# Loading the output weights earlier, and the norm weights and two rows of x later, at the end of attention

## The chip, the cores and the metric

The kernel runs on one core of one Trainium2 chip. The metric is the time of one execution on the device in microseconds (us). TensorE multiplies, VectorE, ScalarE and GpSimd (POOL) work on vectors, and SyncE's queue (SP) issues nearly all transfers between the chip's memory and the core's on-chip memory.

## The reference

One layer of a decoder on 2048 tokens of width 1024, in float32. Cut to what matters here:

```python
nx = rmsnorm(h, attn_norm_g[l])
proj = jnp.einsum('bsd,dp->bsp', nx, w_in[l])
...
o_a = gla_mixer(...)                       # gated linear attention, 4 heads
o_a = o_a * lax.rsqrt(...) * gla_norm_g * jax.nn.silu(gr)
o_b = dilated_mixer(dq, dk_, dv_, rel_bias)  # 8 heads, three branches each, combined
mixed = jnp.concatenate([o_a, o_b], axis=-1)
h = h + jnp.einsum('bsm,md->bsd', mixed, w_out[l])

nm = rmsnorm(h, mlp_norm_g[l])
a = jnp.square(jax.nn.relu(jnp.einsum('bsd,df->bsf', nm, w_ff1[l])))
h = h + jnp.einsum('bsf,fd->bsd', a, w_ff2[l])
return rmsnorm(h, final_norm_g)
```

## The kernel before

Five stages follow one another: the input projection, attention, the output product (from 897 us), the first MLP product and the second MLP product. The big products are done in float32 through three products of split operands: a value is rounded to a high part by ScalarE (`A.activation(..., AF.Copy)`), VectorE subtracts it from the value to get the low part, and TensorE multiplies high by high, low by high and high by low (`mm3`, lines 65 to 68). Whatever enters such a product as a weight needs a load, a ScalarE copy and a VectorE subtraction first; for the output weights these are lines 899, 900 and 901 in `load_wo`, once for each of eight blocks of 128 rows.

**Attention** runs over 160 units, made from 4 pairs of heads, 2 heads in each and 3 branches (dilations 16, 4 and 1) of each head. A unit is four blocks of 128 queries in the branch of dilation 16 and two in the others. The loop does one turn for each unit in a pipeline: the scores of the unit three turns ahead (lines 659 and 661, then bias and minimum on VectorE in line 671 and the exponential on ScalarE in line 672), the transposes of the unit of this turn (line 681, copied out by ScalarE in 688 or VectorE in 690), and the product with v of the unit two turns back (line 700, copied out in 703). The gated linear attention (GLA, lines 827 to 889) goes along in small steps. For the branches of dilation 16 and 4, q is packed by POOL first (`pack_q`, line 613). When a pair of heads is done with a branch its result goes to memory (`boD`, line 777); when all three are done, the rows are loaded again (`combine_load`, line 725, tile `cmb`) and combined by weights (`combine`, lines 737 to 760), by POOL for the first three pairs and half by POOL, half by VectorE for the last. Combined rows and GLA's rows go to `mixD`, also through line 777, except those of the last pair for the first eight tiles, which are read from their tile `O`.

Work that belongs to a certain turn is registered with `at_unit` and done ahead of that turn's own work. `load_wo` is registered for the eight turns 132, 135, ..., 153.

**Output product.** `mix_T(t)` loads the mixer rows (line 1073) and the rows of x (line 1074) of a tile of 128 tokens into a tile `mx`, transposes the mixer rows (line 377) and splits them into `mT`. Tiles are taken in the order 0, 4, 1, 5, ... The next tile's `mix_T` stands ahead of this tile's product. The first two tiles are multiplied in two halves, chunks 0 to 3 and then 4 to 7. Line 1184 adds the rows of x to the product, and `norm_to_T` norms the sum with the repeated row `gM`. The other repeated row, `gF`, is used by `output` at the end of the second MLP product (lines 1268 and 1272).

**Who sets the order.** The first part of the kernel has its order written out by hand. From line 536 on the framework's scheduler arranges each engine's instructions when the kernel is compiled, by a model of the time and with the order of the program as the priority; `keep_in_program_order` pins an instruction behind what stands ahead of it on its engine. On the chip each engine's stream is then fixed, and an instruction that has to wait holds up what stands behind it on its engine; SP's queue is such a stream too. All large tiles (`slot`) are of one size and come from one ring of 25 buffers; a new tile takes the place of one that has seen its last use, and waits for that use.

Of the kernel before, what the change touches and what calls it, by code (L numbers as in the profile page):

```python
# [18 lines left out]
D = 1024  # L19
# [11 lines left out]
AHEAD, LAG = 3, 2  # L31
# [9 lines left out]
def emit(tc, a, stop=99):  # L41
    nc = tc.nc
    V, A, G, T, SP = nc.vector, nc.scalar, nc.gpsimd, nc.tensor, nc.sync
# [6 lines left out]
    def ps(tag):  # L50
        return psum.tile([128, 512], F32, name="ps_" + tag, tag=tag, bufs=BANKS[tag])

    def slot(name, dt=F32, n=SLOT):

        return up.tile([128, SLOT], dt, name=name, tag="u", bufs=25)[:, :n]

    def view(t, shape):
        n = int(np.prod(shape))
        names = "abcd"[:len(shape)]
        return t[:, :n].rearrange(f"p ({' '.join(names)}) -> p {' '.join(names)}", **dict(zip(names, shape)))  # L60

    def bcast_row(ap, n):
        return bass.AP(tensor=ap.tensor, offset=ap.offset, ap=[[0, 128], [1, n]])

    def mm3(out, sh, sl, mh, ml, first, last):
        T.matmul(out, sh, mh, start=first, stop=False)  # L66
        T.matmul(out, sl, mh, start=False, stop=False)  # L67
        T.matmul(out, sh, ml, start=False, stop=last)  # L68
# [82 lines left out]
    x2 = a["x"].rearrange("o s d -> (o s) d")  # L151
# [198 lines left out]
    def split(hi, lo, src):  # L350
        A.activation(hi, src, AF.Copy)  # L351
        V.tensor_tensor(lo, src, hi.bitcast(F32), op=OP.subtract)  # L352
# [18 lines left out]
    def transposed(xt, last=None, pin=False, by=ident):  # L371
        out = []
        for q in range(2):
            pv = view(ps("cd"[q]), (4, 128))
            for k in range(4):
                of = xt[:, (4 * q + k) * 128:(4 * q + k + 1) * 128]
                ins = T.transpose(pv[:, k, :], last if last is not None and 4 * q + k == 7 else of, by)
                if pin and q + k == 0:
                    tc.keep_in_program_order(ins)
            out.append(pv)  # L380
        return out
# [78 lines left out]
    def reload(n):  # L460

        j, cs = order[n // 2], slice(1024 * (n % 2), 1024 * (n % 2) + 1024)
        t = (xp, bp)[n // 2 % 2][:, cs]
        SP.dma_start(t, nTD[j - 1].rearrange("p c s -> p (c s)")[:, cs])

        def rest():
            hi, lo = [v[:, cs] for v in TF[j]]
            tc.keep_in_program_order(A.activation(hi, t, AF.Copy))
            V.tensor_tensor(lo, t, hi.bitcast(F32), op=OP.subtract)
            if n + 4 < 14:  # L470
                back.append(reload(n + 4))

        return rest
# [418 lines left out]
    wo = a["w_out"].rearrange("o (c p) n -> p (o c) n", p=128)  # L892
    WO = []

    def load_wo(n):
        for c in range(len(WO), len(WO) + n):
            raw = slot("woraw")[:, :D]
            w = view(slot("wo", FR), (2, D))
            SP.dma_start(raw, wo[:, c])
            A.activation(w[:, 0], raw, AF.Copy)  # L900
            V.tensor_tensor(w[:, 1], raw, w[:, 0].bitcast(F32), op=OP.subtract)
            WO.append(w)
# [35 lines left out]
    def at_unit(n, *f):  # L938
        plan.setdefault(n, []).append(f)
# [44 lines left out]
            was = b  # L984
    NU = len(units)
    for i in range(8):
        at_unit(NU - 28 + 3 * i + AHEAD, load_wo, 1)
    gla = gla_steps()
    for k in range(-AHEAD, NU + LAG):
# [3 lines left out]
        if 0 <= k - LAG:  # L993
            u = units[k - LAG]
            u.b.v = vs[u.b.h // 2, u.b.br]
            pv = u.values()
        if k + AHEAD < NU:
            u = units[k + AHEAD]
# [9 lines left out]
        if 0 <= k - LAG:  # L1008
            u = units[k - LAG]
# [14 lines left out]

    gs = slot("gs")
    gM, gF = gs[:, :D], gs[:, D:2 * D]
    SP.dma_start(gM, bcast_row(a["mlp_norm_g"], D))
    SP.dma_start(gF, bcast_row(a["final_norm_g"], D))
    bb, tb = slot("bb"), slot("tb")
    rb, TF, TB = [slot("rb")], {}, {}  # L1030

# [37 lines left out]
    def mix_T(t):  # L1069
        u = view(slot("mx"), (2, D))  # L1070
        to = D - 128 if t < 8 else D
        for cs in (slice(0, 512), slice(512, to)) if t in (0, 4) else (slice(0, to),):
            SP.dma_start(u[:, 0, cs], mixD[t * 128:t * 128 + 128, cs])
        SP.dma_start(u[:, 1], x2[t * 128:t * 128 + 128])
        m = view(slot("mT", FR), (2, CH, 128))
        for q, pv in enumerate(transposed(u[:, 0], outs[3, 0][:, t, 1:129] if t < 8 else None)):
            split(*[m[:, i, 4 * q:4 * q + 4] for i in range(2)], pv)
        return u, m
# [38 lines left out]
    def bank():  # L1117
        tags.append(tags.pop(0))
        return ps(tags[-1])

    def product1(at):
        g, j = jobs1[at]
        half, gh = divmod(g, NP)
        if not acc1:
            acc = [slot("acc1") for _ in range(4)]
            acc1.extend(t[:, 512 * q:512 * q + 512] for t in acc for q in range(4))
        X, c11, c12, c21, c22, s2, s4 = acc1[7 * (g % 2):7 * (g % 2) + 7]
        p = bank()
        B, W = TB[j], combs1[at % 4]
        for c in range(4):  # L1130
            mm3(p, W[:, 0, c], W[:, 1, c], B[0][:, c], B[1][:, c], c == 0, c == 3)

        def square(v):
            A.activation(v, v, AF.Relu)  # L1134
            A.activation(v, v, AF.Square)

        def store(q, n, v):
            q.dma_start(actD[n - 1, half, gh], v)

        if j in (1, 5, 4):  # L1140
            A.activation({1: X, 5: c22, 4: c21}[j], p, AF.Copy)
        elif j == 2:
            V.tensor_tensor(c11, p, X, op=OP.add)
            square(c11)
            store(A, 1, c11)
        elif j == 6:
            V.tensor_tensor(X, p, X, op=OP.add)
            V.tensor_tensor(c12, X, c22, op=OP.add)
        elif j == 3:
            V.tensor_tensor(c12, p, c12, op=OP.add)  # L1150
            square(c12)
        else:
            V.tensor_tensor(X, p, X, op=OP.add)
            V.tensor_tensor(c21, c21, X, op=OP.add)  # L1154
            V.tensor_tensor(c22, c22, X, op=OP.add)
            square(c22)
            square(c21)
            store(SP, 4, c22)
            store(SP, 2, c21)
            V.tensor_tensor(X, c12, c22, op=OP.add)  # L1160
            V.tensor_tensor(s2, X, c11, op=OP.subtract)
            V.tensor_tensor(c12, c11, c12, op=OP.subtract)
            V.tensor_tensor(s4, c21, s2, op=OP.subtract)
            for n, v in ((5, X), (6, s2), (7, c12), (3, s4)):
                store(SP, n, v)

    tiles = [8 * half + i + 4 * k for half in range(2) for i in range(4) for k in range(2)]
    nxt = mix_T(tiles[0])
    late = None
    back = []  # L1170
    for at, t in enumerate(tiles):
        u, m = nxt
        if at + 1 < NT:
            nxt = mix_T(tiles[at + 1])
        h = u[:, 1]
        p = [ps("a"), ps("a")]
        parts_ = 2 if at < 2 else 1
        for q in range(parts_):
            for n in range(2):
                cs = slice(n * 512, n * 512 + 512)  # L1180
                for c in range(q * CH // parts_, (q + 1) * CH // parts_):
                    mm3(p[n], m[:, 0, c], m[:, 1, c], WO[c][:, 0, cs], WO[c][:, 1, cs], c == 0, c == CH - 1)
                if q == parts_ - 1:
                    V.tensor_tensor(h[:, cs], p[n], u[:, 1, cs], op=OP.add)
        SP.dma_start(hD[t * 128:t * 128 + 128], h)
        if late is not None:
            norm_to_T(*late)
        if back:
            list(back.pop())
        if at in RELOAD:  # L1190
            back.append(reload(order[at - RELOAD[0]], 0))
        if at == W1AT:
            load_w1(0)
        if at == W1AT + 1:
            prep1(0)
            prep1(1)
        late = (h, u[:, 0], t)
# [144 lines left out]
    for at in range(7, len(jobs1)):  # L1342
        if at == first - 2:
            halves.update({n: reload(order[n], 1) for n in range(2)})
        prep1(at + 2)
        product1(at)
        for n in parts_at.get(at, ()):
            next(halves[n])
            if n in begun and n + 2 < 7:
                halves[n + 2] = reload(order[n + 2], 1)  # L1350
            begun.add(n)
        if at == len(jobs1) - 6:
            for n in range(2):
                load_b(n)
                load_a(n)
        if at in (len(jobs1) - 4, len(jobs1) - 2):
            n = (at + 4 - len(jobs1)) // 2
            prep_b(n)
            prep_a(n)
# [3 lines left out]
    for ph, (j, half) in enumerate(phases):  # L1363
        P = [bank() for _ in range(4)]
        for k in range(8):
            n = 8 * ph + k
            prep_a(n + 2)
            at = k + 8 * (1 - half)
# [72 lines left out]
```

## Time and profile before

| what | value |
|---|---|
| median of 3 runs | 2332.82 us (2329.7 to 2334.34) |
| the profiled execution's own time | 2333.23 us |
| its span, first to last instruction | 2331.4 us |
| instructions | 34990 |
| mean granted TensorE clock | 0.993 |
| transfers | 457.59 MB, 196 GB/s on average |

The profile is one execution. Its page gives the busy time of each engine (PE is TensorE, PEld its weight loads, DVE VectorE, ACT ScalarE, SPq SyncE's queue), and the trace behind it can be asked for stretches of time, for the instructions in order, and for who waited for whom. In a row of the timeline stand the start in us, the duration, the engine, the line of the kernel, the operation with its tiles (out<-in), and in brackets the idle time of the engine just before it and what ended it. In a row of waits stand the waiting engine with its tile and line, the releaser, and the us in total, the number of waits and the longest. In a table of stretches each engine has its busy time and, in brackets, the number of its instructions; the last three columns are the granted TensorE clock (1.00 is full), the busy share of the transfer engines, and GB/s. In a tile's answer a row has the durations in ns (least/median/greatest) and the first and last start.

### The profile page before, as it was taken

The page shows a single profiled execution, that of the slowest core. Times are in us where ns is not written, and L with a number is a line of the kernel's source. Part 1 is how long each engine was busy: PE and PEld are TensorE (multiplying, and loading weights), DVE is VectorE, ACT ScalarE, POOL GpSimd, SP SyncE. Part 2 cuts the span into 40 slices and gives each one's busy share as a digit, 9 for nine tenths or more (in the row PEclk, how much of TensorE's full clock was granted, in tenths as well). Part 3 has the DMA queues.
Part 4 walks back from the last instruction along what each step waited for, and adds up shares of the span by engine and source line. Part 5 has one row for each costly group of instructions (what it writes and reads, how often), then busy time and mean ns, then how long its engine had stood idle before and what let it go on. Part 6 is the DMA issues. An engine that isn't in the chain of part 4 may idle for free.

```text
span 2331.4 us, 34990 instructions
## 1 busy us (share of the span) xinstructions
PE 2289.2 (98%) x12652; PEld 1978.2 (85%) x12652; DVE 1572.1 (67%) x2926; ACT 1146.1 (49%) x2200; POOL 434.2 (19%) x530
## 2 busy tenths in 40 slices
PE   6999999999999999999999999999999999999998
PEld 6977999789999998888888887888888888888886
DVE  7978778776677677445877779777764356446545
ACT  5665446535677673224555566555544223224324
POOL 0133103235377685000000000000000100001002
PEclk9999999999999999999999999999999999999999
DMA  4457754777676855678644447444476487457643
GB/s 152 143 159 239 219 179 127 215 224 237 199 234 210 279 181 187 196 229 277 200 158 155 157 149 269 165 153 156 155 266 230 164 284 251 139 170 261 209 162 108
DMA packets 341804, 457.59 MB, mean 196 GB/s; under 512 B 18117, under 2 KB 214230, under 8 KB 336256
## 3 DMA queue, kind: packets, MB, share of 16 engines
q1 hardware_dynamic: 336878, 446.71, 59.0%
q10 hardware_dynamic: 4754, 8.66, 1.0%
q8 instruction: 99, 1.62, 0.3%
q14 instruction: 73, 0.60, 0.1%
HBM read 292.99 MB, written 167.02 MB: 197 GB/s over the span
## 4 chain that ended last, share of the span: by engine, by line
PE 76%; DVE 2%; DMA 1%; POOL 1%; issue 1%; ACT 1%; SPq 0%; POOLq 0%; DVEq 0%; ACTq 0%
PE ps_a L66 8%; PE ps_a L68 8%; PE ps_a L67 8%; PE ps_c L66 7%; PE ps_c L67 7%; PE ps_c L68 7%; PE ps_d L66 4%; PE ps_d L68 4%; PE ps_d L67 4%; PE ps_a L700 4%; PE ps_o L67 3%; PE ps_o L68 2%; PE ps_o L66 2%; PE ps_d L681 2%; PE ps_c L659 2%; PE ps_c L661 2%
## 5 line engine op out<-in xcount | busy, mean ns | idle before, releaser
L352 DVE TENSOR_TENSOR ca<-ra,ca 128x1024 fp32r<-128x1024 f32 x112 | 137.8, 1231 | 157.5 <-ACT ca L351 157.4
L1268 POOL TENSOR_TENSOR suma<-suma,gs 128x512 f32<-128x512 f32 x16 | 23.3, 1471 | 1144.0 <-ACT scr L1266 1143.9
L351 ACT ACTIVATE ca<-ra 128x1024 fp32r<-128x1024 f32 x112 | 118.0, 1053 | 220.3 <-PE ps_c L68 176.0
L351 ACT ACTIVATE w1comb<-w1raw 128x512 fp32r<-128x512 f32 x224 | 139.7, 627 | 151.8 <-PE ps_c L68 54.6
L352 DVE TENSOR_TENSOR w1comb<-w1raw,w1comb 128x512 fp32r<-128x512 f32 x224 | 154.0, 690 | 49.5 <-ACT w1comb L351 49.2
L672 ACT ACTIVATE pe<-pe,O 128x256 f32<-128x256 f32 (+1 forms) x384 | 156.0, 454 | 61.3 <-DVE O L671 58.1
L700 PE MATMUL ps_a<-v,pt 128*128 128x65 f32 x1200 | 179.7, 253 | 2.4 <-DVE pt L690 2.0
L700 PEld LDWEIGHTS ps_a<-v,pt 128*128 128x128 f32 x1200 | 176.4, 195 | 5.0 <-DVE pt L690 2.6
L681 PE MATMUL ps_d<-ident,pe 128*128 128x128 f32 x600 | 158.5, 279 | 1.1 <-ACT pt L688 1.1
L671 DVE CUSTOM_DVE_ANT_0 pe<-ps_c,nb 128x256 f32<-128x256 f32 (+1 forms) x384 | 126.3, 361 | 37.6 <-PE ps_d L681 15.2
L206 ACT ACTIVATE wcomb<-wraw 128x512 fp32r<-128x512 f32 (+2 forms) x126 | 96.6, 774 | 94.1 <-PE ps_o L67 19.5
L351 ACT ACTIVATE cb<-rb 128x1024 fp32r<-128x1024 f32 x56 | 59.4, 1061 | 163.7 <-PE ps_o L67 105.0
L67 PE MATMUL ps_c<-hb,w1comb 128*128 128x512 f32 x336 | 131.0, 390 | 0.1
L66 PE MATMUL ps_c<-hb,w1comb 128*128 128x512 f32 x336 | 130.8, 389 | 0.0
L68 PE MATMUL ps_c<-hb,w1comb 128*128 128x512 f32 x336 | 130.7, 389 | 0.0
L66 PE MATMUL ps_c<-cb,ca 128*128 128x512 f32 x336 | 130.7, 389 | 0.0
L67 PE MATMUL ps_c<-cb,ca 128*128 128x512 f32 x336 | 130.7, 389 | 0.0
L68 PE MATMUL ps_c<-cb,ca 128*128 128x512 f32 x336 | 130.7, 389 | 0.0
L208 DVE TENSOR_TENSOR wcomb<-wraw,wcomb 128x512 fp32r<-128x512 f32 (+2 forms) x84 | 90.2, 1075 | 31.0 <-ACT wcomb L206 30.8
L681 PEld LDWEIGHTS ps_d<-ident,pe 128*128 128x128 f32 x600 | 108.8, 186 | 1.7 <-ACT pt L688 1.3
L352 DVE TENSOR_TENSOR cb<-rb,cb 128x1024 fp32r<-128x1024 f32 x56 | 68.2, 1222 | 60.6 <-ACT cb L351 60.5
L1134 ACT ACTIVATE acc<-acc 128x512 f32<-128x512 f32 x128 | 79.6, 631 | 52.8 <-DVE acc L1154 34.8
(392 smaller groups left out, 7158.4 us busy)
## 6 DMA issues: line engine op xcount, KB each, us to landing
ra<-actD SPq DMA_DIRECT2D x56, 1024.0 KB, 7.0
actD<-acc SPq DMA_DIRECT2D x192, 256.0 KB, 2.4
rb<-w_ff SPq DMA_DIRECT2D x72, 512.0 KB, 4.5
w1raw<-w_ff SPq DMA_DIRECT2D x32, 1024.0 KB, 5.7
k<-kD SPq DMA_DIRECT2D x16, 1024.0 KB, 8.0
rb<-hTD SPq DMA_DIRECT2D x13, 1024.0 KB, 6.0
wraw<-w_in SPq DMA_DIRECT2D x48, 256.0 KB, 4.1
cmb<-boD SPq DMA_DIRECT2D x16, 528.0 KB, 5.6
```

Of the source, the lines that this page charges most:

```text
L66: T.matmul(out, sh, mh, start=first, stop=False)
L67: T.matmul(out, sl, mh, start=False, stop=False)
L68: T.matmul(out, sh, ml, start=False, stop=last)
L206: A.activation(hi, src, AF.Copy, scale=sc)
L208: V.tensor_tensor(lo, src, hi.bitcast(F32), op=OP.subtract)
L351: A.activation(hi, src, AF.Copy)
L352: V.tensor_tensor(lo, src, hi.bitcast(F32), op=OP.subtract)
L671: V.tensor_tensor_reduce(p, s, bias, scale=1.0, scalar=BIG, op0=OP.add, op1=OP.min, accum_out=nm)
L672: A.activation(p, p, AF.Exp, bias=nm, scale=-1.0)
L681: T.transpose(pb[:, i * 128:i * 128 + 128], src, ident)
L700: T.matmul(self.b.opsum[:, n % 4], self.pt[:, i * 128:i * 128 + 128], self.b.v[:, blk, cols], start=first, stop=last)
L1134: A.activation(v, v, AF.Relu)
```

## The change

The load of each block of output weights is taken out of `load_wo` and registered by itself eight turns earlier, so for turns 124, 127, ..., 145. The repeated row `gM` is loaded behind the first tile's `mix_T`, and `gF` in the first MLP product, behind its product number 14, pinned to that place in SP's queue. For the first two tiles (0 and 4) `mix_T` no longer loads the rows of x; they are loaded in the loop, behind the next tile's `mix_T`.

```diff
+    wo_raw = {}
+
+    def raw_wo(c):
+        wo_raw[c] = slot("woraw")[:, :D]
+        SP.dma_start(wo_raw[c], wo[:, c])
+
     def load_wo(n):
         for c in range(len(WO), len(WO) + n):
-            raw = slot("woraw")[:, :D]
+            raw = wo_raw.pop(c)
             w = view(slot("wo", FR), (2, D))
-            SP.dma_start(raw, wo[:, c])
             A.activation(w[:, 0], raw, AF.Copy)
             V.tensor_tensor(w[:, 1], raw, w[:, 0].bitcast(F32), op=OP.subtract)
             WO.append(w)
...
     for i in range(8):
+        at_unit(NU - 36 + 3 * i + AHEAD, raw_wo, i)
         at_unit(NU - 28 + 3 * i + AHEAD, load_wo, 1)
...
     gM, gF = gs[:, :D], gs[:, D:2 * D]
-    SP.dma_start(gM, bcast_row(a["mlp_norm_g"], D))
-    SP.dma_start(gF, bcast_row(a["final_norm_g"], D))
...
-        SP.dma_start(u[:, 1], x2[t * 128:t * 128 + 128])
+        if t not in (0, 4):
+            SP.dma_start(u[:, 1], x2[t * 128:t * 128 + 128])
...
     nxt = mix_T(tiles[0])
+    SP.dma_start(gM, bcast_row(a["mlp_norm_g"], D))
...
         if at + 1 < NT:
             nxt = mix_T(tiles[at + 1])
+        if at < 2:
+            SP.dma_start(u[:, 1], x2[t * 128:t * 128 + 128])
...
         product1(at)
+        if at == 14:
+            tc.keep_in_program_order(SP.dma_start(gF, bcast_row(a["final_norm_g"], D)))
```

## The prediction

> **What bounds the kernel now.** I read the page first: TensorE is busy over the whole span, so time can only be won where it stands or runs slowly. Then a table of stretches around the end of attention, the only place that the change touches before 900 us.
>
> ```profile
> PE 2289.2 (98%) x12652; PEld 1978.2 (85%) x12652; DVE 1572.1 (67%) x2926; ACT 1146.1 (49%) x2200; POOL 434.2 (19%) x530
> ...
> core 0: us, PE busy (x) PEld busy (x) DVE busy (x) ACT busy (x) POOL busy (x), PEclk, DMA share, GB/s
> 840.00:860.00 20.00, 19.93 (x182) 19.52 (x181) 17.35 (x55) 15.79 (x40) 19.84 (x23) 1.00 0.68 223
> ...
> 860.00:865.00 5.00, 3.57 (x33) 3.13 (x32) 2.52 (x10) 3.55 (x10) 5.00 (x5) 1.00 0.79 260
> 865.00:872.00 7.00, 6.75 (x32) 6.08 (x31) 5.92 (x18) 5.09 (x14) 6.68 (x9) 0.51 0.73 186
> ...
> 884.00:890.00 6.00, 4.94 (x40) 4.37 (x40) 6.00 (x10) 3.95 (x13) 6.00 (x5) 1.00 1.03 393
> 890.00:892.40 2.40, 0.63 (x6) 0.39 (x4) 2.40 (x4) 1.09 (x2) 2.24 (x3) 0.98 0.40 155
> 892.40:895.80 3.40, 3.38 (x17) 3.38 (x18) 3.40 (x8) 0.00 (x0) 3.40 (x3) 0.51 0.00 0
> 895.80:905.00 9.20, 9.20 (x62) 8.36 (x62) 6.36 (x13) 2.59 (x6) 8.57 (x18) 1.00 0.45 138
> ```
>
> The columns after the stretch are its length and each engine's busy time. There are two holes. The first: TensorE is idle 5.00 - 3.57 = 1.43 us in 860 to 865 and 0.25 us up to 872, together 1.68, and then works 7.00 us at a granted clock of 0.51, which costs 7.00 x 0.49 = 3.43. Sum **5.11 us**. The second: idle 6.00 - 4.94 = 1.06, 1.77 and 0.02 us, and 3.40 x 0.49 = 1.67 of half clock, **4.52 us**. From these two at most 9.63 us can come. Before and after them the rows have TensorE full.
>
> What ends the first hole is told by the timeline, the queue of SyncE beside it, and the table of waits (us in total, times, longest).
>
> ```profile
> 855.99 0.37 SPq L777 DMA_DIRECT2D mixD<-O  x1
> 856.41 0.57 SPq L899 DMA_DIRECT2D woraw<-w_out  x1
> 859.13 0.37 SPq L777 DMA_DIRECT2D boD<-O  x1
> 859.59 0.42 SPq L899 DMA_DIRECT2D woraw<-w_out  x1
> ...
> 866.58 6.28 SPq L725 DMA_DIRECT2D cmb<-boD  x4
> ...
> 861.42 1.06 ACT L900 ACTIVATE wo<-woraw 128x1024 fp32r<-128x1024 f32 x1 [1.90 <-DMA woraw<-w_out]
> ...
> 866.46 1.04 ACT L900 ACTIVATE wo<-woraw 128x1024 fp32r<-128x1024 f32 x1
> ...
> 862.51 1.51 DVE L901 TENSOR_TENSOR wo<-woraw,wo 128x1024 fp32r<-128x1024 f32 x1 [2.48 <-ACT wo L900]
> ...
> 863.02 0.44 PE L870 MATMUL ps_o<-ident,gla 128*128 128x128 f32 x2 [1.09 <-ACT gla L862]
> ...
> ACT wo L900 <- DMA woraw<-w_out: 4.9, 4, 1.9
> ...
> SPq L899 <- PE ps_c L661: 8.6, 2, 8.3
> ...
> SPq L725 <- DVE wo L901: 3.9, 1, 3.9
> ```
>
> The fifth weight row was issued at 856.41, straight behind the store of a combined pair, and ScalarE reached its split before it landed: 1.90 us of waiting with everything behind it in line (the GLA copy L862, for which TensorE waits). VectorE waits 2.48 us for ScalarE's half, and so do its bias sums and copies of transposed probabilities. Of four such waits (4.9 us) only this one shows in TensorE's rows.
>
> ```profile
> 883.62 1.26 DVE L901 TENSOR_TENSOR wo<-woraw,wo 128x1024 fp32r<-128x1024 f32 x1
> ...
> 887.69 2.93 DVE L758 TENSOR_TENSOR cmb<-cmb,small 128x512 f32<-128x512 f32 x2
> 890.55 1.21 DVE L901 TENSOR_TENSOR wo<-woraw,wo 128x1024 fp32r<-128x1024 f32 x1
> ...
> 892.42 0.69 PE L700 MATMUL ps_a<-v,pt 128*128 128x65 f32 x2 [1.78 <-DVE pt L690]
> ```
>
> The second hole has no transfer in it. VectorE is busy 6.00 of 6.00 and 2.40 of 2.40 us: two late splits and the combination of the last pair stand before the copy that TensorE needs.
>
> **The change part by part.** No arithmetic is added or removed; all of it is order.
>
> *Weight rows eight turns earlier.*
>
> ```profile
> L899 SPq DMA_DIRECT2D woraw<-w_out x8: 333/382/578, 830.0 to 878.9; - x8
> ...
> DMA to landing us min/median/max: 3.5/5.0/5.3
> ```
>
> Eight loads, three turns apart, take 830.0 to 878.9: 48.9 / 21 = 2.33 us a turn, so eight turns are 18.6 us against a landing of at most 5.3. The wait of L900 for its DMA goes in all four places. In the first hole that takes away the cause: 1.68 us idle, and the half clock that follows, 3.43. I take **-5.11**. Bounds: 0, if another wait holds the same split; -5.11 at the other end, since nothing else stands in the rows there. The eight issues (0.38 us each) only change places in SyncE's queue.
>
> The clock is worth a remark, as two thirds of this term are clock. The row shows half clock right behind an idle time of 1.68 us and again behind 1.77. [...]
>
> *What it costs: slots.* Every large tile comes from one ring of 25 slots, and slots are given in program order: the two rows of norm weights, which wait for no data, go out only behind the last weight row.
>
> ```profile
> 876.47 0.58 SPq L899 DMA_DIRECT2D woraw<-w_out  x1
> ...
> 878.86 0.55 SPq L899 DMA_DIRECT2D woraw<-w_out  x1
> 879.65 0.33 SPq L1027 DMA_DIRECT2D gs<-mlp_norm_g  x1
> 880.03 0.50 SPq L1028 DMA_DIRECT2D gs<-final_norm_g  x1
> 880.63 0.93 SPq L1073 DMA_DIRECT2D mx<-mixD  x2
> ```
>
> The ring is full in this stretch. The first weight row waits 8.3 us for the scores to be done with a packed q (L661), and the combine loads L725 wait 3.9 us for a split (L901), that is for a weight row's slot. I count the tiles alive at 866: 4 of GLA, pe, pt, one bias, one v (8), q and two k of both heads (14), the older pair's result and its combine tile (16), the last pair's result (17), six split weights (23), two combine tiles (25). A raw row now lives about eight turns instead of two or three, so two or three more are held. Early on (800 to 830 us) this pushes the packing of q (L613) towards the scores that need it. VectorE and TensorE have three turns of lead there, 7 us, against casts of four parts that can start once the q of the branch before is free; I take **0** and bound it by +1.7, the idle time of the first hole. Near the end the sixth and seventh row hold the slots of the two combine tiles:
>
> ```profile
> 873.21 2.53 POOL L760 TENSOR_TENSOR O<-O,cmb 128x512 f32<-128x512 f32 x2
> ...
> 875.11 0.65 DVE L737 TENSOR_TENSOR small<-O,cmb 128x8 f32<-128x8 f32 x1
> ...
> 895.36 0.42 PE L377 MATMUL ps_d<-ident,O 128*128 128x128 f32 x1
> ...
> 897.72 0.48 PE L66 MATMUL ps_a<-wo,mT 128*128 128x512 f32 x1
> ```
>
> Then L725 has to wait until POOL lets the older combine tile go, at 873.21 + 2.53 = 875.7: up to 875.7 - 866.6 = 9.1 us later. Combining starts at 875.11 and reaches TensorE at 895.36, 20 us, with VectorE and POOL doing other work in between; some of it can close up, and the first tile's first half product (24 matmuls from 897.72) doesn't need it. Bounds: 0 and +9.1; I take **+1.5**, near the low end, since most of the 20 us is queueing.
>
> *Second hole.* If splits wait for no transfer, the last two can run before VectorE is taken up by combining. The two subtractions are 1.26 + 1.21 = 2.47 us, more than the 1.77 us of idle; gone, with their half clock, this is 1.77 + 1.67 = 3.44. If splits bunch up here instead, nothing is won. Half way: **-1.7**; bounds 0 and -3.44.
>
> *Norm weights and x rows later.* 512 KB each for the two repeated rows and for two rows of x leave the place ahead of, or among, the first tiles' mixer rows.
>
> ```profile
> mx<-x SPq DMA_DIRECT2D x2, 512.0 KB, 8.6
> boD<-O SPq DMA_DIRECT2D x2, 528.0 KB, 4.1
> ...
> L1184 DVE TENSOR_TENSOR mx<-ps_a,mx x32: 679/691/692, 911.5 to 1100.3; 128x512 f32<-128x512 f32 x32
> ...
> L1268 POOL TENSOR_TENSOR suma<-suma,gs x16: 1267/1304/2343, 1843.5 to 2324.6; 128x512 f32<-128x512 f32 x16
> ```
>
> The mixer rows land a few us earlier, but TensorE's first transpose of them stands behind other work, not behind a transfer, so this wins **0** by itself; it is what lets a faster attention run on into the product. The x rows are first read at 911.5; issued some 10 us later, by 899, and landing within 8.6, they are in time. If they were not, TensorE still has the next tile's product before it lacks a PSUM bank. The final norm's row is first read at 1843.5 and is now issued early in the first MLP stage, hundreds of us ahead: 0. Bounds for both: 0 and +1.7, one idle of the first hole's size.
>
> **Sum.** -5.11 + 0 + 1.5 - 1.7 + 0 = -5.3. The profiled execution took 2333.23 us (span 2331.4 and 1.8 around it), 0.4 above the median 2332.82; so 2333.23 - 5.3 = 2327.9 in its terms, and **2327.5** beside the median.
>
> **The rivals.**
>
> *The wait moves.* The load is early but the split's own slot isn't free: with the raw rows holding slots, the fifth split needs the one that the store boD<-O at 859.13 gives back when it has landed (4.1 us in the row above), no sooner than the 861.42 at which it ran before. For it: the waits of L899 and L725 on slots; the same store line in front of both. Against: splits are then placed where their slot is free, and may not block ScalarE at the same spot. Nothing net: 2332.8, and 2330 to 2335 around it. This is also how the change would fail to do what it says.
>
> *Slower: the split waits for POOL.* The sixth split's slot comes free only with POOL's last L760 at 875.7, where before its load went out at 859.59 and its split ran at 866.46. If ScalarE's queue reaches it on time, it stands up to 875.7 - 866.5 = 9.2 us, the exponentials behind it; three turns of lead cover little, as the first hole's 1.90 us wait already made 1.68 us idle. That is some 9 us idle and 3.4 us of half clock, less the 5.11 won and part of the second hole: 12.4 - 5.1 - 1 = +6, 2339. It decides from a wait of about 5 us on. For it: POOL is busy 19.84 of 20.00 and 5.00 of 5.00 us in the rows from 840 to 865. Against: a schedule that counts POOL's time puts the split behind it.
>
> *Clock not tied to the gap.* If the half clock came from something else than this idle time, only the idle would go: -1.68 - 0.9 (half of 1.77) + 1.5 = -1.1, 2331.7 beside the median. The rows speak against it: 0.51 stands behind both gaps and nowhere else here. [...]
>
> *Both holes close* and combining isn't late: -5.11 - 3.44 = -8.6, 2324.2.
>
> **How the numbers follow.** The forecast, with both holes' case as its good end, has 0.42; the moved wait 0.25 and the untied clock 0.05, both within 0.2% (about 4.7 us, what a measurement of this kernel can tell from no change); the slower case 0.28. So faster 0.42, same 0.30, slower 0.28. As cases of both signs matter, the range runs from below the best case to the slower case and a little over: 2321 to 2341. The forecast's own range is 2323 to 2331.
>
> **What would show it.** Right: L900 waits for no DMA; TensorE's row for the fifth split has no idle time and the clock stays 1.00 through 865 to 872; the combine loads still come before 870. Wrong: L900 waiting for a store, for PE or for POOL; L725 near 876 and the transposes of O after 900 with idle TensorE before them; the packing of q ending a wait of the scores.

## The result, and the profile after

The changed kernel takes **2340.51 us** in the median of 5 runs (2336.17 to 2342.72), the kernel before 2332.82 (2329.7 to 2334.41, 5 runs). The ratio is **1.0031, 95% interval 1.002 to 1.0043**: some 7 us slower, where 5 us faster was forecast. One execution of a kernel described further down, h1, took 6030.16 us; its ratio leaves that one out. The profiled execution of the changed kernel took 2342.72 us with a span of 2340.9, against 2331.4 before. In its listing the split is in lines 905 (ScalarE) and 906 (VectorE) instead of 900 and 901, and the addition of x in line 1192 instead of 1184; the load is in line 899 of both.

Not all of the 9.5 us between the two spans belongs to the change. The last store that SyncE issues ahead of the first moved load stands in the timeline of its queue at 805.63 before and at 808.07 after:

```profile
805.63 0.36 SPq L777 DMA_DIRECT2D mixD<-O  x1
```

```profile
808.07 0.36 SPq L777 DMA_DIRECT2D mixD<-O  x1
809.10 5.03 SPq L899 DMA_DIRECT2D woraw<-w_out  x1
...
862.70 0.33 SPq L899 DMA_DIRECT2D woraw<-w_out  x1
...
870.74 0.33 SPq L899 DMA_DIRECT2D woraw<-w_out  x1
...
880.60 4.03 SPq L725 DMA_DIRECT2D cmb<-boD  x4
```

So 2.4 us were there before the change could act: up to that place both traces have the same instructions in the same order on every engine. The additions of x, 911.5 to 1100.3 in the row quoted for the forecast, are now here (line 1192's instructions: durations in ns, first and last start):

```profile
L1192 DVE TENSOR_TENSOR mx<-ps_a,mx x32: 675/691/692, 919.1 to 1107.5; 128x512 f32<-128x512 f32 x32
```

The last one is 7.2 us later, so 7.2 - 2.4 = **4.8 us** arose between 808 and 1107; the other 2.3 came behind 1107, where nothing but the one load of `gF` differs in the order of the instructions. What was bought for the 4.8 is in the answer for the tile of raw weights:

```profile
L899 SPq DMA_DIRECT2D woraw<-w_out x8: 332/333/5026, 809.1 to 870.7; - x8
L905 ACT ACTIVATE wo<-woraw x8: 1042/1058/1059, 847.9 to 880.9; 128x1024 fp32r<-128x1024 f32 x8
L906 DVE TENSOR_TENSOR wo<-woraw,wo x8: 1216/1226/2211, 849.0 to 887.0; 128x1024 fp32r<-128x1024 f32 x8
its engine sat idle before it (us, times) until:
  ACT wo L905: 2.0, 3
  DVE wo L906: 1.3, 1
  POOL O L760: 0.3, 1
```

Before, the same answer had the loads at 830.0 to 878.9 and the eight ScalarE halves at 833.5 to 884.4. The first load is 20.9 us earlier, and no split waits for its load any more; yet the **first split is 14.4 us later** (847.9 against 833.5; 2.4 of it is the shift). In the built program the first split went into the place of an old bias tile before. With raw rows ahead of it in the ring, the last packed q now takes that place, and the first split gets the place of this packed q, which the scores read until 846.9. Four splits bunch up at 848 to 861 us. Two stalls follow. The first is in the timeline of VectorE and TensorE:

```profile
859.40 0.43 DVE L703 COPY O<-ps_a 128x260 f32<-128x260 f32 x1 [2.61 <-PE ps_a L700]
860.57 1.28 DVE L906 TENSOR_TENSOR wo<-woraw,wo 128x1024 fp32r<-128x1024 f32 x1 [0.74 <-ACT wo L905]
861.89 0.29 DVE L671 CUSTOM_DVE_ANT_0 pe<-ps_c,nb 128x128 f32<-128x128 f32 x1
...
862.59 0.39 PE L659 MATMUL ps_c<-k,qs 128*128 128x256 f32 x1 [2.94 <-DVE O L671]
```

The row at 861.89 is the first bias sum of the last pair's plain branch (dilation 1); it stood at 852.32 before. Here it stands straight behind the fourth split, and TensorE, whose next scores wait for that sum, is idle for 2.94 us. In the built program the tile `O0`, into which this sum also writes, takes the place of the **fourth raw row**, whose last use is that split; before, it took the third's, which was free much sooner (its split ends at 851.52). The fourth split in turn is written into the place of an old v, released by the product L700 for which VectorE waits in the first row. So the chain is: L700 (it ends at 859.36), split (ScalarE, from 859.50), split (VectorE), bias sum, scores. ScalarE comes to this split only at that time anyway, behind work that itself waited for TensorE (its L862 at 858.56, 3.30 us).

The second stall is where the combination meets the output product. In a table of stretches (length, each engine's busy time, clock):

```profile
845.00:862.60 17.60, 14.42 (x125) 13.73 (x123) 12.53 (x30) 12.53 (x32) 17.44 (x17) 1.00 0.80 283
862.60:880.00 17.40, 17.05 (x150) 16.55 (x151) 15.89 (x56) 14.72 (x36) 17.01 (x18) 1.00 0.57 170
880.00:884.75 4.75, 2.85 (x29) 2.64 (x27) 0.43 (x2) 3.16 (x7) 1.00 (x3) 1.00 0.82 214
884.75:891.60 6.85, 6.28 (x29) 5.91 (x30) 6.19 (x20) 3.95 (x13) 1.84 (x5) 0.50 1.17 327
891.60:903.60 12.00, 10.31 (x97) 9.97 (x96) 11.47 (x33) 6.71 (x21) 9.04 (x19) 1.00 0.64 241
903.60:920.00 16.40, 13.44 (x66) 10.85 (x67) 14.95 (x28) 1.90 (x4) 14.31 (x19) 1.00 0.07 17
```

TensorE's idle time is 3.18 + 0.35 + 1.90 + 0.57 + 1.69 + 2.96 = 10.65 us, and half clock over 6.85 us costs 3.4: 14.1 us, against 9.63 in the two holes before, 4.4 of the 4.8 us. Who ends the later idle times is in the timeline again:

```profile
884.75 0.17 DVE L737 TENSOR_TENSOR small<-O,cmb 128x8 f32<-128x8 f32 x1 [3.84 <-DMA cmb<-boD]
885.32 0.58 PE L659 MATMUL ps_c<-k,qs 128*128 128x256 f32 x1 [2.47 <-DVE O L671]
...
903.54 0.50 PE L66 MATMUL ps_a<-wo,mT 128*128 128x512 f32 x1 [1.69 <-DVE O L703]
...
914.21 3.24 DVE L758 TENSOR_TENSOR cmb<-cmb,gla 128x512 f32<-128x512 f32 x2
917.97 1.16 DVE L760 TENSOR_TENSOR O<-O,cmb 128x512 f32<-128x512 f32 x1
919.06 0.68 DVE L1192 TENSOR_TENSOR mx<-ps_a,mx 128x512 f32<-128x512 f32 x1
...
919.79 0.50 PE L66 MATMUL ps_a<-wo,mT 128*128 128x512 f32 x1 [2.35 <-DVE mx L1192]
```

The combine loads, at 866.58 before, are issued at 880.60, behind the eighth raw row at 870.74. In the built program one of the two combine tiles takes the place of the older pair's result, which its last store has to let go, and the other that of the sixth raw row. In the waits of SyncE's queue this is

```profile
SPq L777 <- POOL O L760: 9.9, 3, 4.3
...
SPq L725 <- DMA mixD<-O: 2.1, 1, 2.1
```

so POOL's combining of the older pair holds up the stores, and the stores hold up the loads. VectorE stands 3.84 us for the loads and holds up the scores at 885.32; then its half of the combination runs at 914 to 919, ahead of the first addition of x, and TensorE waits 2.35 us for that addition, which reads a finished product out of the memory that TensorE writes (PSUM).

### The profile page after: what moved, and what is told of

Its sections match the earlier page's. It is cut to its first block, busy times and chain, and to the rows that moved or that the text cites. A ratio compares the mean times of both kernels' runs of the same rounds, so it can differ in the third digit from the quotient of the medians.

```text
span 2340.9 us, 34995 instructions
## 1 busy us (share of the span) xinstructions
PE 2290.9 (98%) x12652; PEld 1978.5 (85%) x12652; DVE 1570.6 (67%) x2926; ACT 1145.7 (49%) x2200; POOL 432.0 (18%) x530
## 4 chain that ended last, share of the span: by engine, by line
PE 48%; DVE 1%; DMA 1%; ACT 1%; issue 0%; POOL 0%; POOLq 0%; SPq 0%; DVEq 0%; ACTq 0%
PE ps_c L67 6%; PE ps_c L66 6%; PE ps_c L68 6%; PE ps_a L67 4%; PE ps_a L68 4%; PE ps_a L66 4%; PE ps_d L66 4%; PE ps_d L67 4%; PE ps_d L68 4%; PE ps_o L67 2%; PE ps_o L68 2%; PE ps_o L66 2%; DMA rb<-w_ff 1%; DMA rb<-hTD 1%; DVE cb L352 0%
## 5 line engine op out<-in xcount | busy, mean ns | idle before, releaser
L700 PE MATMUL ps_a<-v,pt 128*128 128x65 f32 x1200 | 179.0, 252 | 0.6 <-DVE pt L690 0.6
L700 PEld LDWEIGHTS ps_a<-v,pt 128*128 128x128 f32 x1200 | 175.8, 195 | 2.5 <-DVE pt L690 1.0
L351 ACT ACTIVATE cb<-rb 128x1024 fp32r<-128x1024 f32 x56 | 59.4, 1061 | 166.9 <-PE ps_o L67 90.4
L66 PE MATMUL ps_a<-wo,mT 128*128 128x512 f32 x256 | 101.2, 396 | 4.0 <-DVE mx L1192 2.4
```

Of the source, the lines that this page charges most:

```text
L700: T.matmul(self.b.opsum[:, n % 4], self.pt[:, i * 128:i * 128 + 128], self.b.v[:, blk, cols], start=first, stop=last)
```

## The experiments

Theory **S**, formed from these rows: raw rows held for eight turns take ring slots which (a) the plain branch's result `O0` and (b) the last pair's combine tiles need. Rival **M**: the moved norm weights and x rows cost the time. Rival **W**: the loads just aren't early enough or in the right place. Each kernel was timed in five rounds beside the kernel before, and its ratio has a 95% interval. "First sums" is the time from the first bias sum of the unit 24 units ahead of the plain branch (793.28 us before) to the plain branch's first one (852.32), so that an execution's own shift drops out. "L725" is when the last pair's combine loads are issued, two times where they are issued in two groups; the shift, from -1.3 to +3.9 us against before, is still in it. The ratio is to the kernel before in the same rounds, which took 2333.46 us beside e1 to e4, 2332.37 beside g1 to g4 and 2333.24 beside h1 to h5. The g kernels ran on another chip than the e and h kernels; the full loss was not measured on that one.

| kernel | median us | ratio to before | first sums, us | L725, us |
|---|---|---|---|---|
| before | 2332.82 | 1 | 59.0 | 866.6 |
| changed | 2340.51 | 1.0031 (1.002 to 1.0043) | 66.2 | 880.6 |
| e1_weights_only | 2339.5 | 1.0036 (1.0023 to 1.0048) | 66.3 | 877.1 |
| e2_moves_only | 2333.74 | 1.0003 (0.9994 to 1.0012) | 59.6 | 871.0 |
| e3_last_two_late | 2336.3 | 1.0014 (1.0005 to 1.0023) | 66.2 | 869.4, 873.4 |
| e4_lead_two | 2334.81 | 1.0011 (1.0003 to 1.002) | 59.2 | 873.0, 877.7 |
| g1_slots_held | 2334.59 | 1.0007 (0.9998 to 1.0016) | 59.4 | 875.8 |
| g2_pairs | 2334.64 | 1.0009 (1.0 to 1.0018) | 56.2 | 868.7 |
| g3_first_four_early | 2332.93 | 0.9997 (0.9988 to 1.0006) | 62.2 | 865.5, 869.7 |
| g4_last_four_early | 2333.08 | 1.0003 (0.9994 to 1.0012) | 62.8 | 877.6, 880.1 |
| h1_o0_first | 2331.65 | 0.9988 (0.9979 to 0.9997) | 60.0 | 873.4, 877.9 |
| h3_rows_split | 2331.14 | 0.9988 (0.9979 to 0.9997) | 62.4 | 867.8, 871.9 |
| h4_held_early | 2336.77 | 1.0016 (1.0007 to 1.0025) | 64.1 | 874.9 |
| h5_held_both | 2339.82 | 1.0025 (1.0016 to 1.0034) | 64.4 | 880.5 |

### The parts of the change alone

**e1** takes the early weight rows only (`raw_wo`, its use in `load_wo`, and the registration eight turns ahead); norm weights and x rows are where they were. **e2** takes the rest only.

> Only the weight rows go eight turns earlier; norm weights and x rows as in the kernel before. Theory S (the raw rows hold the slots of the ring that the last pair's plain-branch result O0 and its combine tiles cmb need): the bias sums of that branch start near 862 us as in the changed kernel (852 before), the combine loads L725 go out after 875 us (866.6 before), and the time is 2337 to 2343 us. Rival M (the moved x rows and norm weights cost the time, by delaying the first tiles): 2329 to 2334 us, no slower than before.

> Weight rows loaded at their split as before; only the norm weights and the x rows of tiles 0 and 4 go later. Theory S: L725 at about 866.6 us, 2329 to 2334 us, the same as before. Rival M: 2337 to 2343 us, as the changed kernel, with TensorE waiting for the line that adds the x rows.

All of the loss is with the weight rows; the moves are worth nothing, and M falls. The timeline of e1 (addition of x in its line 1190) has the stalls of the changed kernel, the first of the same length (2.94 us), and VectorE late with the first addition of x:

```profile
857.02 1.28 DVE L906 TENSOR_TENSOR wo<-woraw,wo 128x1024 fp32r<-128x1024 f32 x1 [0.74 <-ACT wo L905]
858.33 0.29 DVE L671 CUSTOM_DVE_ANT_0 pe<-ps_c,nb 128x128 f32<-128x128 f32 x1
...
859.03 0.58 PE L659 MATMUL ps_c<-k,qs 128*128 128x256 f32 x1 [2.94 <-DVE O L671]
...
917.47 0.49 PE L66 MATMUL ps_a<-wo,mT 128*128 128x512 f32 x1 [3.08 <-DVE mx L1190]
```

In e2 the mixer rows do end an idle time of TensorE, against what the forecast said of them, but the total doesn't show it:

```profile
890.28 0.63 PE L377 MATMUL ps_c<-ident,mx 128*128 128x128 f32 x4 [2.05 <-DMA mx<-mixD]
```

### Fewer turns, fewer rows

In **e3** rows 6 and 7 go behind the combine loads, in **e4** all rows have a lead of two turns (both on the changed kernel):

```diff
-        at_unit(NU - 36 + 3 * i + AHEAD, raw_wo, i)
+        at_unit((NU - 36 + 3 * i if i < 6 else NU - 10) + AHEAD, raw_wo, i)   # e3
+        at_unit(NU - 30 + 3 * i + AHEAD, raw_wo, i)                           # e4
```

> The changed kernel, but the seventh and eighth weight rows are loaded in turn 150, behind the combine loads of the last pair. Theory S: the combine loads come back to before 872 us (880.6 in the changed kernel), and the half-clock time near 885 us and the late O transposes go; the late O0 slot (bias sums near 862 us) stays. 2331 to 2337 us. Rival M, and any rival that doesn't lie in the combine tiles: 2338 to 2343 us, as the changed kernel.

> The changed kernel with a lead of two turns in place of eight. Theory S: at two turns no row is loaded ahead of the split before it except the seventh, ahead of the combine loads; O0 gets its slot as before (bias sums near 852 us), and one of the two halves of the combine loads goes out some 10 us late. 2331 to 2338 us, between the two kernels. Rival M: as the changed kernel, 2338 to 2343 us. Rival W (the loads' own waits were what mattered, and an earlier load is better the earlier it is): slower than the changed kernel's eight turns.

e3 brings the combine loads back and keeps the late sums; about half of the loss goes, and the 2.94 us stay. So does the wait for the first addition of x, with 3.50 us: it goes with the late sums, not with late combine loads.

```profile
863.13 0.39 PE L659 MATMUL ps_c<-k,qs 128*128 128x256 f32 x1 [2.94 <-DVE O L671]
...
916.65 0.50 PE L66 MATMUL ps_a<-wo,mT 128*128 128x512 f32 x1 [3.50 <-DVE mx L1192]
```

e4 has the sums on time and keeps a little loss. W is refuted: in e4 less lead costs less. But neither run separates (a) from (b) for good.

**g3** and **g4**, on the kernel before, give the lead of eight turns to rows 0 to 3 or to rows 4 to 7 alone:

```diff
+        at_unit(NU - (36 if i < 4 else 28) + 3 * i + AHEAD, raw_wo, i)   # g3
+        at_unit(NU - (28 if i < 4 else 36) + 3 * i + AHEAD, raw_wo, i)   # g4
```

> Weight rows 0 to 3 loaded eight turns ahead, rows 4 to 7 with their split; norm weights and x rows as before. Theory S (only rows that stand ahead of the last pair's tiles cost, and those held when these are asked for): bias sums of the plain branch at most 2 us later than the 59, L725 at 867 to 873, 2333 to 2335. Rival T (each moved load costs its share): half of the loss of all eight, 2336 to 2337.

> Weight rows 4 to 7 loaded eight turns ahead, rows 0 to 3 with their split; norm weights and x rows as before. Theory S: nearly the whole loss, L725 at 874 to 879, bias sums of the plain branch 3 to 7 us later than the 59, 2337 to 2341. Rival T: half of the loss, 2336 to 2337.

g3 came out nearly as S said: its sums are 3.2 us late where 2 were allowed, and it costs nothing. **g4 missed**: nearly the whole loss was expected, and there is none, although its combine loads are as late as in the changed kernel:

```profile
877.61 1.00 SPq L725 DMA_DIRECT2D cmb<-boD  x2
878.70 1.30 SPq L777 DMA_DIRECT2D mixD<-gla  x1
880.09 1.77 SPq L725 DMA_DIRECT2D cmb<-boD  x2
```

What it lacks is the other stall: its plain branch starts ahead of the fourth split, not behind it.

```profile
855.19 0.28 DVE L671 CUSTOM_DVE_ANT_0 pe<-ps_c,nb 128x128 f32<-128x128 f32 x1
...
858.25 1.32 DVE L906 TENSOR_TENSOR wo<-woraw,wo 128x1024 fp32r<-128x1024 f32 x1 [1.18 <-ACT wo L905]
```

So late combine tiles alone don't cost the time, nor do moved transfers as such (the rival T of these runs), nor sums that are 3 to 4 us late (62.2 and 62.8), and rows 0 to 3 plus rows 4 to 7 are not the sum of their parts: 0 and 0, together 1.0036. That turned S into **S2**: the late plain branch carries the loss, and late combining adds to it only then. Its rival C is that late combining carries most of it after all, and the rest was luck of the clock.

### Two rows in one slot

**g2** loads two raw rows into one slot, on the kernel before, with a lead of two turns, rows 6 and 7 in turn 150 behind the combine loads:

```diff
+    def raw_wo(c):
+        both = view(slot("woraw"), (2, D))
+        SP.dma_start(both, wo[:, c:c + 2])
+        wo_raw[c], wo_raw[c + 1] = both[:, 0], both[:, 1]
...
+        if i % 2 == 0:
+            at_unit((NU - 30 + 3 * i if i < 6 else NU - 10) + AHEAD, raw_wo, i)
```

> The kernel before with the raw weight rows loaded two in one slot: rows 0 and 1, 2 and 3, 4 and 5 two turns ahead of the first one's split, rows 6 and 7 in turn 150 behind the combine loads; the norm weights and x rows as before. Theory S: the last pair's tiles take their slots no later than before, L725 at 864 to 870, bias sums of the plain branch 59 us behind unit 120's; splits wait for no transfer; 2327 to 2333, faster if the gap at 861 us goes. Rival T or W (a load ahead of its split costs by itself): 2335 or more, as with the lead of two turns.

The sums are the earliest of all (56.2 us) and L725 is on time, as S said, but the median, 2334.64, is above the range given. "Splits wait for no transfer" did not hold. One idle time of 4.38 us of TensorE stands in its profile, with these rows ahead of it:

```profile
872.71 1.74 SPq L899 DMA_DIRECT2D woraw<-w_out  x1
...
881.13 2.00 ACT L906 ACTIVATE wo<-woraw 128x1024 fp32r<-128x1024 f32 x2 [3.90 <-DMA woraw<-w_out]
...
883.36 0.84 DVE L887 TENSOR_TENSOR gla<-gla,ps_o 64x256 f32<-64x256 f32 x2
...
884.31 1.21 PE L827 MATMUL ps_o<-gla 128*128 128x130 f32 x4 [4.38 <-issue]
```

The last row names no releaser. In the built program L827 waits for the GLA sum L887, which ends at 884.20. On VectorE that sum stands behind a split, the split waits for ScalarE's half, and ScalarE waits 3.90 us for the last pair of rows, issued at 872.71. So this kernel brings in a wait for a late load of its own, and its time says nothing for or against S.

### Slots held by nothing

If slots are what costs, a kernel that only holds slots must lose the time too. **g1**, **h4** and **h5** are the kernel before, in which slots are taken by one write of POOL and given back by a copy of one column that reads the latest split; no load is moved in the program. g1 holds two in turns 142 and 145 to 150 and 153, h4 two in turns 127 and 128 to 141, h5 all four.

```diff
+    def hold():
+        held.append(slot("held")[:, :1])
+        G.memset(held[-1], 0.0)
+
+    def let_go():
+        V.tensor_copy(held.pop(0), WO[-1][:, 1, :1].bitcast(F32))
```

> The kernel before with two ring slots taken in turns 142 and 145, written once by POOL, and given back in turns 150 and 153; no load, split or row is moved in the program. Theory S (the slots held early cost the time): the last pair's combine loads L725 come at 875 to 879 as in the changed kernel, the bias sums of the first plain-branch unit stay about 59 us behind those of unit 120 (their slot is taken earlier in the program), 2335 to 2339. Rival T (the transfers moved into 809 to 871 us, or the moved splits, cost it): nothing of that is here, 2332 to 2334.

> The kernel before with two ring slots held by no transfer, taken in turns 127 and 128 and given back behind the fourth split (turn 141); loads, splits and rows are where they were in the program. Theory S2: the plain branch's scores late (65 us or more behind unit 120's), combine tiles about as before, 2334 to 2337, as with the last two rows loaded late. Rival C: 2332 to 2334.

> The same two slots held in turns 127 to 141, and besides the two of the first held kernel (turns 142 and 145 to 150 and 153): no transfer moved ahead. Theory S2: both late, the loss of the changed kernel without any of its moves: bias sums 65 us or more behind unit 120's, L725 at 875 to 881, 2337 to 2341. Rival C: 2334 to 2336, the first held kernel's time. Rival T (the moved transfers): 2332 to 2334.

Before S was changed, g1 was to cost 2 to 6 us; it cost 1.0007, and its interval includes 1, with L725 at 875.8: again late combining alone is cheap. The times of h4 and h5 came out as S2 said, their sums at 64 where 65 or more was expected. But h4's combine loads, expected about as before, come 8.3 us later (6.2 without the shift), so h4 too has both lates. With the late sums of about 64 us h5 loses nearly what the changed kernel loses, with no row loaded ahead. They are not pure copies of its stall, though. In both built programs `O0` takes an old v's place and not a raw row's. Holding slots made the loads late as well (the first at 841.9 instead of 830.0), and the larger idle time of h5 is the old one of the fifth split's load (ScalarE, then TensorE):

```profile
862.04 1.06 ACT L900 ACTIVATE wo<-woraw 128x1024 fp32r<-128x1024 f32 x1 [2.30 <-DMA woraw<-w_out]
...
863.45 0.48 PE L681 MATMUL ps_d<-ident,pe 128*128 128x128 f32 x1 [2.87 <-ACT pe L672]
```

They show that slots alone can make such a loss, not by which stall the changed kernel makes it.

### The one slot

**h1** is that test: the whole changed kernel, in which `O0` asks for its slot a little earlier, by one write of POOL ahead of the sixth raw row (row 5; the text put on record calls it the fifth). The element written is overwritten when the product with v is copied out (L703).

```diff
+    def o0_first():
+        outs[3, 0] = view(slot("O0"), (NT, 132))
+        G.memset(outs[3, 0][:, 0, :1], 0.0)
+
+    at_unit(NU - 21 + AHEAD, o0_first)
```

> The changed kernel, in which the last pair's plain-branch result O0 asks for its slot some turns earlier (one element of it written by POOL ahead of the fifth raw row), so that it takes the third raw row's slot and not the fourth's; the combine tiles still come as late as in the changed kernel. Theory S2 (the loss needs both lates together: first scores of the plain branch behind the fourth split, and combining late): bias sums of the plain branch 62 us or less behind unit 120's, no idle of 2.9 us ahead of its scores, L725 still at 875 to 881, 2333 to 2336. Rival C (the late combine tiles alone carry most of it, the other runs were luck of the clock): 2338 to 2341.

The median goes to 2331.65, 0.9988 of before (0.9979 to 0.9997): **the whole loss is gone, and the change is now a small gain**, more than S2 said (2333 to 2336). Rival C, which asked for 2338 to 2341, falls. In the built program `O0` now takes the third raw row's place. In the timeline of VectorE the first sum stands right behind the third split, 8.7 us sooner than in the changed kernel (6.2 without the shift). The fourth split, which now gets the place that a store of `boD` lets go, comes far behind it:

```profile
851.88 1.23 DVE L906 TENSOR_TENSOR wo<-woraw,wo 128x1024 fp32r<-128x1024 f32 x1
853.14 0.29 DVE L671 CUSTOM_DVE_ANT_0 pe<-ps_c,nb 128x128 f32<-128x128 f32 x1
...
865.37 1.88 DVE L906 TENSOR_TENSOR wo<-woraw,wo 128x1024 fp32r<-128x1024 f32 x1 [0.80 <-ACT wo L905]
```

In the stretches TensorE is now full where it lost 3.18 us, and what is left lies at the end:

```profile
845.00:862.60 17.60, 17.30 (x157) 16.93 (x156) 14.50 (x46) 15.37 (x40) 17.28 (x21) 1.00 0.65 222
862.60:880.00 17.40, 16.42 (x145) 15.58 (x143) 14.36 (x45) 13.02 (x27) 14.12 (x14) 1.00 0.72 218
880.00:892.80 12.80, 9.89 (x82) 8.81 (x80) 12.35 (x37) 6.42 (x21) 9.31 (x21) 1.00 1.07 354
892.80:899.70 6.90, 6.72 (x21) 5.40 (x20) 6.26 (x17) 0.92 (x3) 6.57 (x10) 0.51 0.31 120
```

Idle 0.30 + 0.98 + 2.91 + 0.18 = 4.37 us and 6.90 x 0.49 = 3.38 of half clock: 7.8 us, against 9.63 before and 14.1 in the changed kernel.

One request thus undoes the loss, but it moves more than one tile: every slot given out behind it changes, part of the combine loads come earlier (873.4) than the 875 to 881 expected, and the scheduler orders the instructions anew, as it does for every kernel here. Which share of the 10 us between h1 and the changed kernel belongs to the late sums alone is not shown.

**h3** reaches the same another way: rows 0 to 3 eight turns ahead, 4 and 5 two turns, 6 and 7 behind the combine loads, on the changed kernel.

```diff
-        at_unit(NU - 36 + 3 * i + AHEAD, raw_wo, i)
+        at_unit((NU - 36 if i < 4 else NU - 30 if i < 6 else NU - 10 - 3 * i) + 3 * i + AHEAD, raw_wo, i)
```

> The changed kernel (norm weights and x rows late) with rows 0 to 3 eight turns ahead, rows 4 and 5 two turns ahead, rows 6 and 7 in turn 150 behind the combine loads. Theory S2: bias sums of the plain branch 62 us behind, L725 at 866 to 872, neither late, 2329 to 2333. Rival C: also not late, 2330 to 2334; a rival by which any early row costs: 2336 or more.

2331.14, also 0.9988. With these two the change beats the kernel before, by some 3 us as the ratios have it (0.7 to 4.9 us by their intervals).

## Why the prediction was wrong

It went wrong chiefly at one step of the sum, the early slots, which were put at 0 with a bound of +1.7. With that stall gone (h1) the change gains about 3 of the 5.3 us forecast.

- **Views of before.** That the ring is full at 866 us, that slots go out in order and that raw rows would hold two or three more of them was read rightly, and it is where the loss comes from.
- **Slots early: the step that failed.** The forecast named one taker of slots there, the packing of q, and gave it three turns of cover. That packing did move (its last eight casts start at 820.4 to 837.6 instead of 812.4 to 822.1), and no score waited for it. The takers that mattered were the splits themselves (first one 14.4 us later) and `O0`, which is written by a bias sum that has no cover: TensorE's scores stand behind it. There are 2.94 us of idle time at the place, where +1.7 was the bound, and more behind it, since a plain branch that starts late ends late. h1 measures the term: between 1.0031 and 0.9988 lie 0.0043 x 2333 = 10 us, with everything that follows from it, the earlier combine loads included.
- **First hole, -5.11.** The mechanism was right: no split waits for its load, and the hole doesn't open in h1, where 0.30 us are idle up to 862.6. In the changed kernel a new stall opens at the same place, so nothing of it is won.
- **Combine tiles late, +1.5 of 0 to +9.1.** L725 was to come at most 9.1 us later; it came 14.0 later, 11.6 without the shift of 2.4. The price by itself is in keeping with the runs: g4 and g1, with L725 at 876 to 880, cost 0.0003 and 0.0007, 0.7 and 1.6 us, neither clear of zero. On top of late scores it is more: e1 against e3, 1.0036 against 1.0014, is 5 us, though e3 keeps two rows back as well.
- **Second hole, -1.7.** Not won: splits do bunch up, only earlier (848 to 861 us), and the combination still ends late.
- **Norm weights and x rows, 0.** e2 measures 1.0003 (0.9994 to 1.0012).
- **The slower rival.** It gave 2339, close to what came, by another way: the sixth split was to wait some 9 us for POOL. The tile's answer has 0.3 us of waiting for POOL's L760. So that 2340.51 lies in the wide range of 2321 to 2341 is luck, and the time is no evidence for this rival; its root, a slot that frees too late, was the right one, at the wrong tile. The rival of the moved wait had the same root, the split's own slot, and put it at nothing net.
- **What would show it wrong** named a late L725 and idle TensorE ahead of the work after 900 us, and both came; but a late L725 by itself is cheap (g1, g4), and it came dear only together with late scores. The forecast asked which *transfer* and which *split* loses its slot, and never listed the tiles that are first written in this stretch by the engines on the path.

## What to carry to other kernels

When a load is made earlier in a kernel whose tiles share one ring, write down every tile that is first written between the new and the old place, and whose slot each one gets then: the price can fall on a tile that comes next in order, here one that TensorE waited for, and not on the load. A split or cast that frees the raw tile needs a slot too, so loading far ahead can make it later. If one tile on the path gets the bad slot, letting that tile ask first (here one small write) can keep the early load and lose the stall.

## What the runs showed of the hardware

How long an idle time of TensorE is doesn't decide by itself whether half clock follows. Two kernels have the same idle time of 2.94 us for the same instruction. In the changed kernel the stretch behind it, 862.60 to 880.00, has the clock at 1.00; in e1 it is this:

```profile
858.00:864.90 6.90, 5.87 (x28) 5.87 (x29) 5.11 (x26) 5.49 (x15) 6.75 (x9) 0.51 0.36 115
```

That is 6.90 x 0.49 = 3.4 us of price for the same event, or none. In the changed kernel half clock came at 884.75 instead, behind an idle time of 1.90 us. In the tables of stretches shown here half clock lasts 6.85 us in the changed kernel, 6.90 in e1 and h1, and 7.00 and 3.40 in the kernel before: about 3.4 us of price each, and 1.7 for the last one. What decides whether it follows is not shown, and no run was made to place a gap.

So a difference of some 3 us between two single profiles of this kernel can be the clock alone, which is why the verdicts here rest on the ratios over all rounds.
